# A hybrid decoder layer on one core: output projection in three rounds, triangular solve in smaller steps, and other priorities for weight splits and bank evictions

## The chip, the cores and the metric

The kernel runs on one core of one Trainium2 chip. The metric is the device time of one execution in microseconds (us); the figure of a kernel is the median of its runs. One more execution was taken with the hardware profiler, and all rows below are of that one.

## The reference

One decoder layer for 256 tokens of width 2048, in float32:

```python
n = rmsnorm(x, attn_norm)
u = n @ w_in                                  # 6928 columns, cut into four groups
mix = concat[gated_deltanet(u_gdn), mlstm(u_mlstm), rglru_block(u_rglru), rwkv7(u_rwkv)]
x = x + mix @ w_out
n = rmsnorm(x, ffn_norm)
x = x + (silu(n @ ffn_w_gate) * (n @ ffn_w_up)) @ ffn_w_down
return rmsnorm(x, final_norm)
```

The four mixers are causal recurrences over the 256 tokens, each 512 wide with four heads (the RWKV-7 one with eight). GatedDeltaNet and RWKV-7 are computed in chunks, for which a unit lower triangular system is solved: here blocks of 32 x 32 are inverted by forward substitution, and the larger blocks are put together with small matmuls.

## The kernel before, in words

**Units.** All large weights are read in units of 128 x 1024 floats (512 KB), in the order in which they are used: 108 units of `w_in` (27 groups of 256 columns, four units each), 32 units of `w_out`, 176 of the gate and up weights and 88 of the down weights, 404 in all. I call them U0 to U403. For each unit `weights` (line 261) issues a DMA into one of 4 buffers `raw` on SP's queue, and `halves` makes from it, into one of 4 buffers each, `whi` (rounded, ScalarE) and `wlo` (the rest, VectorE). `mm3` (line 281) then multiplies in three passes: whi by the high half of the activation, whi by its low half, wlo by its high half. A unit of `w_in` takes 24 matmuls of 256 columns, all others 12 of 512 columns.

**Mixers beside the weights.** A mixer half is a Python generator (`rwkv_half`, `gdn_half`, `mlstm_half`, `rglru_half`), and so are `gates_mm` and the two solves (`joint_solve` over `solve_blocks`). After each unit `tick(TICKS)` adds 0.65 of a step, and at each whole step every living generator goes on to its next `yield`. So a `yield` is a place where the rest of a mixer is put later in program order, by about one and a half units. A generator that waits for another (`while "gdS" not in em.mix: yield`) asks again at each step. The finished output of a half stands in `em.mix[mixer, half]`.

**Order on the queues.** The order of each engine's queue isn't written by hand. A scheduler orders instructions by priority, which is the place in program order, lowered by an offset inside `high_priority(offset=...)`, and by when it thinks that their inputs and buffers are there. `weights` gives the DMA and both splits an offset of PRIO (20 instructions); functions marked `@evict` (`conv`, `silu2`, `shift_mix`, `gelu2`: the emptying of a PSUM bank of a group and what follows) have EPRIO (40); the mixers' matmuls and transposes go through `Lag`, which puts them 20 instructions later. On the chip each queue then runs in that fixed order.

**The output projection.** `w_out` (line 1181) computes four column quarters q of 512. For the quarter it takes the two banks of its 256 tokens, and for each `part` (a half of a mixer) one unit: if the part isn't split yet, it is split into a high and a low half (`split`, lines 1176 and 1177), then 12 matmuls follow and a tick. At the end the two banks are added to the residual `em.xq` (line 1211). There are two passes over the quarters: `early` with RWKV, RG-LRU and GatedDeltaNet (6 units per quarter, U108 to U131) and `late` with mLSTM (2 units per quarter, U132 to U139). While generators live, `bank` gives only the 3 banks `big`; afterwards it goes around all 8.

**Steps in program order around the change.** Counting ticks in the code: GatedDeltaNet's two halves are spawned behind U59 and U75, and the inputs of its solve are complete at U87. The solve `gds` has 31 columns of two VectorE instructions each, 8 columns to a step, and ends at U94. The halves go on and finish at U107 and U109. The second mLSTM half is spawned behind U107 and finishes at U117.

Of the kernel before, what the change touches and what calls it, by code (L numbers as in the profile page):

```python
# [23 lines left out]
TICKS = 0.65  # L24
LAG = 20
UNIT = 1024
PRIO = 20
EPRIO = 40
WARM = 14
TAIL = 3  # L30
HOLD = {("rw1", 17): 1, ("gates", 1): 1, ("rg0", 0): 1, ("rg1", 1): 3}
# [758 lines left out]
def gates_mm(em):  # L790
# [5 lines left out]
    z = em.mx()  # L796
# [47 lines left out]
    nc.vector.tensor_tensor_scan(M[0:4, 0:T], M[0:4, T : 2 * T], M[0:4, T : 2 * T], 0.0, op0=ALU.max, op1=ALU.max)  # L844
    em.Md = em.dp.tile([4, T], F32, name="Md", tag="Md")
    nc.sync.dma_start(em.Md, M[0:4, 0:T])
    t = em.mx()
    for a in range(2):
        em.pe.transpose(t[:, a * 4 : a * 4 + 4], M[0:4, a * P : a * P + P], em.ident[0:4, 0:4])
# [17 lines left out]
def gdn_half(em, hf, Q, K, V, SZ):  # L867
# [3 lines left out]
    for s, X, bias in ((1, Q, em.c_lnq), (0, K, 0.0)):  # L871
        silu2(em, X)
        sq = em.S()
        nc.scalar.activation(sq, X, AF.Square)
        z = yield from sums(em, em.onesr, sq)
        rsqrt_ln(em, sq, z, em.c_4eps, ebias=bias)
        nc.vector.tensor_tensor(KQv[:, s, :], X, sq, op=ALU.mult)
        em.free(sq, X)
        yield
    silu2(em, V)  # L880
    z = em.mx()
# [25 lines left out]
    for g in range(2):  # L907
        z = em.mx()
# [132 lines left out]
def mlstm_half(em, hf, Q, K, V1, SO, v1s):  # L1041
    nc = em.nc
    silu2(em, Q)
    silu2(em, K)
    while "gates" not in em.mix:
        yield
    zb = bcast_rows(em, em.Md, hf)
    yield
    Hs = em.S(c="B")
    ss = em.const([P, 2, 2], em.nm("mss"))  # L1050
    rs = em.const([P, 2, 2], em.nm("mrs"))
    for g in range(2):
        hd = 2 * hf + g
        E = em.S(c="B")
        nc.vector.tensor_scalar(E[:, 0:T], zb[:, g * T : g * T + T], em.c[:, 0, hd : hd + 1], 0.0, op0=ALU.subtract, op1=ALU.max)
        nc.vector.tensor_scalar(E[:, T : T + P], zb[:, g * T + P : g * T + T], em.c[:, 1, hd : hd + 1], 0.0, op0=ALU.subtract, op1=ALU.max)
        nc.scalar.activation(E[:, 0 : T + P], E[:, 0 : T + P], AF.Exp, scale=-1.0)
        Ed = E.rearrange("p (b n) -> p b n", n=T)[:, :, 0:P]
        nc.vector.tensor_tensor(Ed, Ed, em.incl.unsqueeze(1).to_broadcast([P, 2, P]), op=ALU.mult)
        z = em.mx()  # L1060
        em.pe.matmul(z[:, 0:T], K[:, g * T : g * T + P], Q[:, g * T : g * T + T], start=True, stop=True)
        em.pe.matmul(z[:, T : T + P], K[:, g * T + P : g * T + T], Q[:, g * T + P : g * T + T], start=True, stop=True)
        nc.vector.scalar_tensor_tensor(E[:, 0 : T + P], z[:, 0 : T + P], 0.25 * 128.0**-0.5, E[:, 0 : T + P], op0=ALU.mult, op1=ALU.mult)
        yield
        z = em.mx()
        sq = Seq(em)
        sq.mm(z[:, 0:129], E[:, 0:P], V1[:, 0, g, :], start=True, stop=True)
        sq.mm(z[:, 129:258], E[:, P:T], V1[:, 0, g, :], start=True, stop=False)
        sq.mm(z[:, 129:258], E[:, T : T + P], V1[:, 1, g, :], start=False, stop=True)
        em.free(E)  # L1070
        dn = em.const([P, 2], em.nm("dn"))
        zv = z[:, 0:258].rearrange("p (a n) -> p a n", a=2)
        nc.scalar.activation(dn, zv[:, :, 128], AF.Abs)
        nc.vector.tensor_tensor(dn, dn, em.enm[:, :, hd], op=ALU.max)
        nc.vector.reciprocal(dn, dn)
        junk = em.S(c="B")
        for a in range(2):
            o = slice(g * T + a * P, g * T + a * P + P)
            nc.vector.scalar_tensor_tensor(Hs[:, o], zv[:, a, 0:P], dn[:, a : a + 1], SO[:, a * T + g * P : a * T + g * P + P], op0=ALU.mult, op1=ALU.mult)
            nc.scalar.activation(junk[:, 0:P], Hs[:, o], AF.Square, accum_out=ss[:, g, a : a + 1])  # L1080
        em.free(junk)
        nc.vector.tensor_scalar(ss[:, g], ss[:, g], 1.0 / 128, EPS, op0=ALU.mult, op1=ALU.add)
        nc.gpsimd.tensor_tensor(rs[:, g], ss[:, g], em.mhalf[:, 0:2], op=ALU.pow)
        for a in range(2):
            o = slice(g * T + a * P, g * T + a * P + P)
            nc.scalar.activation(Hs[:, o], Hs[:, o], AF.Copy, scale=rs[:, g, a : a + 1])
        yield
    em.free(Q, K, zb, v1s, SO)
    z = em.mx()
    for u in range(4):  # L1090
        em.pe.transpose(z[:, u * P : u * P + P], Hs[:, u * P : u * P + P], em.ident)
    for g in range(2):
        nc.scalar.activation(Hs[:, g * T : g * T + T], z[:, g * T : g * T + T], AF.Copy, scale=em.PT["mlstm_norm"][:, 2 * hf + g : 2 * hf + g + 1])
    em.mix["ml", hf] = Hs
# [83 lines left out]
    return hi, lo  # L1178


def w_out(em):
    nc, A = em.nc, em.A
    xin = A["x"].rearrange("(a p) d -> p a d", p=P)
# [6 lines left out]
    row = {"gd": 0, "ml": 4, "rg": 8, "rw": 12}  # L1190
    sp = {}

    def run(q, parts):
        banks = [em.bank(), em.bank()]
        for i, (m, hf) in enumerate(parts):
            if (m, hf) not in sp:
                while (m, hf) not in em.mix:
                    em.tick()
                sp[m, hf] = split(em, em.mix[m, hf])
                em.free(em.mix[m, hf])  # L1200
            hi, lo = (t.bitcast(F32R) for t in sp[m, hf])
            whi, wlo = em.weights("w_out", row[m] + 2 * hf, 2, q * 512, 512)
            for a in range(2):
                for kk in range(2):
                    ts = slice(kk * T + a * P, kk * T + a * P + P)
                    em.mm3(banks[a], hi[:, ts], lo[:, ts], whi[:, kk, :], wlo[:, kk, :], start=i == 0 and kk == 0, stop=i == len(parts) - 1 and kk == 1)
            em.tick(TICKS)
            if q == 3:
                em.free(*sp[m, hf])
        for a in range(2):  # L1210
            nc.vector.tensor_tensor(em.xq[a, q], em.xq[a, q], banks[a], op=ALU.add)

    early = [(m, h) for m in ("rw", "rg", "gd") for h in range(2)]
    late = [("ml", 0), ("ml", 1)]
    for q in range(4):
        run(q, early)
    ss = em.const([P, 2, 4], "ss1")

    def norm(q):
# [4 lines left out]
            em.free(junk)  # L1224

    for q in range(4):
        run(q, late)
        if q:
            norm(q - 1)

# [124 lines left out]
def hybrid(tc, A, out, dbg=None, parts=("rw", "gd", "ml", "rg", "tail", "ffn")):  # L1355
    nc = tc.nc
    with ExitStack() as ctx:
# [50 lines left out]
        if "gd" in parts:  # L1408
            for hf in range(2):
                z = grp(GD + 1536 + 256 * hf, tm=True)  # L1410
                SZ = em.S(c="L")
                with em.tc.high_priority(offset=EPRIO):
                    for a in range(2):
                        nc.scalar.activation(SZ[:, a * T : a * T + T], z[:, a * T : a * T + T], AF.Copy, scale=em.rs0[:, a : a + 1])
                silu2(em, SZ)
                Q, K, V = (conv(em, grp(GD + 512 * i + 256 * hf), em.PT["gdn_conv"], 12, (4 * i + 2 * hf, 4 * i + 2 * hf + 1)) for i in range(3))
                em.spawn(f"gd{hf}", gdn_half(em, hf, Q, K, V, SZ))
                if hf == 0:
                    em.spawn("gds", joint_solve(em, "gd", 64, 32, 8, True))
        if "ml" in parts:  # L1420
            for hf in range(2):
                v1s = em.S(2)
# [40 lines left out]
```

## Time and profile before

| | |
|---|---|
| median of 3 runs | 1279.06 us (1278.2 to 1281.37) |
| the profiled execution, own time | 1279.74 us |
| its span, first to last instruction | 1278.0 us |
| TensorE matmul (PE) busy | 1246.7 us, 98% |
| TensorE weight load (PEld) busy | 1077.1 us, 84% |
| VectorE (DVE) busy | 781.3 us, 61% |
| ScalarE (ACT) busy | 636.3 us, 50% |
| mean granted TensorE clock | 0.986 |

The span runs from the first to the last instruction; the own time has 1.7 us more around it. Busy is time in which an engine has an instruction running. Matmuls are pipelined, so that the spacing of their starts, not their duration, is what one costs. L276 is line 276 of the kernel; where a helper passes calls on, many instructions share its line (L276 for what `ch` calls, L401 and L405 for the mixers' matmuls and transposes). [...]

### The profile page before, as it was taken

To read this page: it belongs to the slowest core of one execution; us is meant where nothing else is said; L and a number is where in the kernel's file an instruction comes from. 1 tells how busy PE (TensorE), PEld (TensorE's weight loads), DVE (VectorE), ACT (ScalarE), POOL (GpSimd) and SP (SyncE) were. 2 spreads that over 40 slices of the span, in tenths; PEclk is the share of its full clock that TensorE was granted. 3 is DMA by queue.
4 is the path that set the end of the run, shared out by engine and by line. 5 is a ranking of instruction groups with operands and counts; after the bars stand their busy time and mean duration, and the time that the engine had idled before them with its cause. 6 is when DMAs were issued, how large, how long until landed. Compare 5 with 4: busy or idle time off the path is not lost.

```text
span 1278.0 us, 18349 instructions
## 1 busy us (share of the span) xinstructions
PE 1246.7 (98%) x7216; PEld 1077.1 (84%) x7216; DVE 781.3 (61%) x1082; ACT 636.3 (50%) x846; POOL 31.6 (2%) x65
## 2 busy tenths in 40 slices
PE   9999999999989799999999999999999999999997
PEld 8999999888989688888888888888888888878885
DVE  7676899567798665754444454444454455557554
ACT  7566675517634354644444444444444454445443
POOL 2000000000000100000000000000000000001000
PEclk9999999989999899999999999999999999999999
DMA  9644446234644246666666665666566666666663
GB/s 371 215 129 136 158 124 175 93 120 165 196 145 141 94 149 192 183 181 187 195 188 187 187 196 186 208 199 196 184 194 190 189 185 194 195 191 189 193 190 112
DMA packets 72198, 226.97 MB, mean 178 GB/s; under 512 B 15752, under 2 KB 16016, under 8 KB 72112
## 3 DMA queue, kind: packets, MB, share of 16 engines
q1 hardware_dynamic: 71504, 224.14, 57.0%
q0 software_dynamic: 464, 1.57, 0.4%
q8 instruction: 56, 0.92, 0.3%
q14 instruction: 30, 0.25, 0.1%
q10 hardware_dynamic: 144, 0.10, 0.0%
HBM read 222.49 MB, written 3.28 MB: 177 GB/s over the span
## 4 chain that ended last, share of the span: by engine, by line
PE 87%; DVE 7%; ACT 3%; issue 2%; DMA 1%; POOL 0%; SPq 0%; DVEq 0%; POOLq 0%; ACTq 0%
PE big L171 13%; PE big L170 13%; PE big L169 13%; PE mx L169 10%; PE mx L171 10%; PE mx L170 10%; PE mx L401 4%; PE mxl L171 3%; PE mxl L170 3%; PE mxl L169 3%; DVE wlo L276 2%; PE big L279 2%; DVE sD L494 1%; DVE sD L495 1%; DVE sA L759 1%
## 5 line engine op out<-in xcount | busy, mean ns | idle before, releaser
L276 DVE TENSOR_TENSOR wlo<-raw,whi 128x1024 fp32r<-128x1024 f32 x396 | 485.0, 1227 | 373.5 <-ACT whi L276 371.6
L276 ACT ACTIVATE whi<-raw 128x1024 fp32r<-128x1024 f32 x396 | 418.0, 1057 | 459.9 <-PE big L171 266.9
L171 PE MATMUL big<-nhi,wlo 128*128 128x256 f32 x608 | 176.6, 291 | 1.0 <-DVE wlo L276 1.0
L170 PE MATMUL big<-nlo,whi 128*128 128x256 f32 x608 | 176.5, 290 | 0.0
L169 PE MATMUL big<-nhi,whi 128*128 128x256 f32 x608 | 175.9, 289 | 0.2 <-ACT whi L276 0.2
L170 PE MATMUL big<-wlo,nhi 128*128 128x512 f32 (+1 forms) x464 | 161.8, 349 | 0.0
L171 PE MATMUL big<-whi,nlo 128*128 128x512 f32 (+1 forms) x464 | 161.4, 348 | 0.0
L169 PE MATMUL big<-whi,nhi 128*128 128x512 f32 (+1 forms) x464 | 161.2, 347 | 0.0
L169 PE MATMUL mx<-whi,nhi 128*128 128x512 f32 x352 | 138.0, 392 | 0.0
L171 PE MATMUL mx<-whi,nlo 128*128 128x512 f32 x352 | 137.0, 389 | 0.0
L170 PE MATMUL mx<-wlo,nhi 128*128 128x512 f32 x352 | 137.0, 389 | 0.0
L171 PEld LDWEIGHTS big<-nhi,wlo 128*128 128x128 f32 x608 | 117.6, 194 | 3.5 <-DVE wlo L276 1.2
L170 PEld LDWEIGHTS big<-nlo,whi 128*128 128x128 f32 x608 | 117.5, 193 | 2.8 <-issue 1.3
L169 PEld LDWEIGHTS big<-nhi,whi 128*128 128x128 f32 x608 | 117.4, 193 | 2.6 <-issue 0.7
L170 PEld LDWEIGHTS big<-wlo,nhi 128*128 128x128 f32 x464 | 88.9, 192 | 10.9
L169 PEld LDWEIGHTS big<-whi,nhi 128*128 128x128 f32 x464 | 88.7, 191 | 10.8
L171 PEld LDWEIGHTS big<-whi,nlo 128*128 128x128 f32 x464 | 88.7, 191 | 10.7
L169 PE MATMUL mx<-whi,sA 128*128 128x512 f32 x212 | 82.9, 391 | 0.7 <-ACT sA L1176 0.7
L170 PE MATMUL mx<-wlo,sA 128*128 128x512 f32 x212 | 82.5, 389 | 0.0
L171 PE MATMUL mx<-whi,sA 128*128 128x512 f32 x204 | 79.4, 389 | 0.0
L171 PEld LDWEIGHTS mx<-whi,nlo 128*128 128x128 f32 x352 | 66.1, 188 | 13.8
L170 PEld LDWEIGHTS mx<-wlo,nhi 128*128 128x128 f32 x352 | 66.1, 188 | 13.3
(432 smaller groups left out, 1703.3 us busy)
## 6 DMA issues: line engine op xcount, KB each, us to landing
raw<-in_units SPq DMA_DIRECT2D x404, 512.0 KB, 3.7
sD<-in_x SPq DMA_DIRECT2D x8, 512.0 KB, 7.8
sD<-in_xT SPq DMA_DIRECT2D x4, 512.0 KB, 6.1
out_y<-sD SPq DMA_DIRECT2D x8, 256.0 KB, 3.0
sA<-in_final_norm POOLq DMA_DIRECT2D x4, 256.0 KB, 5.1
sD<-in_lora SPq DMA_DIRECT2D x1, 512.0 KB, 7.1
sD<-in_rglru POOLq DMA_DIRECT2D x1, 512.0 KB, 7.6
dr<-sD SPq DMA_DIRECT2D x2, 256.0 KB, 4.0
```

Source lines behind the costliest of these rows:

```text
L169: i = nc.tensor.matmul(out, ahi, bhi, start=start, stop=False, skip_group_check=True)
L170: nc.tensor.matmul(out, ahi, blo, start=False, stop=False, skip_group_check=True)
L171: self.last_mm = nc.tensor.matmul(out, alo, bhi, start=False, stop=stop, skip_group_check=True)
L276: i = fn(*a, **k)
L279: i = fn(*a, **k)
L401: return self.em.nc.tensor.matmul(*a, **k)
L494: nc.vector.tensor_tensor(tv, col, row, op=ALU.mult)
L495: nc.vector.tensor_tensor(inv[:, j + 1 : n, 0:b], inv[:, j + 1 : n, 0:b], tv, op=ALU.add)
L759: nc.vector.scalar_tensor_tensor(o[:, d:T], u[:, 0 : T - d], tap[3 - d], o[:, d:T], op0=ALU.mult, op1=ALU.add)
```

## The change

Two constants; one more `yield` in `gates_mm`, in `mlstm_half` and (through `sums(..., 1)`) twice in each `gdn_half`; the GatedDeltaNet solve with 4 columns to a step in place of 8; and `w_out` in three passes (rounds) over the quarters in place of two: first RWKV and RG-LRU (4 units per quarter, U108 to U123), then mLSTM (U124 to U131), then GatedDeltaNet (U132 to U139). A part is now split one part ahead of its use, in the last quarter of a round also the first part of the next round.

```diff
-PRIO = 20
-EPRIO = 40
+PRIO = 200
+EPRIO = 100
...
     nc.sync.dma_start(em.Md, M[0:4, 0:T])
+    yield
     t = em.mx()
...
         nc.scalar.activation(sq, X, AF.Square)
-        z = yield from sums(em, em.onesr, sq)
+        z = yield from sums(em, em.onesr, sq, 1)
...
     zb = bcast_rows(em, em.Md, hf)
-    yield
+    for _ in range(2):
+        yield
...
+ROUNDS = ([("rw", 0), ("rw", 1), ("rg", 0), ("rg", 1)], [("ml", 0), ("ml", 1)], [("gd", 0), ("gd", 1)])
...
-    def run(q, parts):
+    def ready(m, hf):
+        if (m, hf) not in sp:
+            while (m, hf) not in em.mix:
+                em.tick()
+            sp[m, hf] = split(em, em.mix[m, hf])
+            em.free(em.mix[m, hf])
+
+    def run(q, r):
+
+        parts = ROUNDS[r]
         banks = [em.bank(), em.bank()]
         for i, (m, hf) in enumerate(parts):
-            if (m, hf) not in sp:
-                while (m, hf) not in em.mix:
-                    em.tick()
-                sp[m, hf] = split(em, em.mix[m, hf])
-                em.free(em.mix[m, hf])
+            ready(m, hf)
+            if i + 1 < len(parts):
+                ready(*parts[i + 1])
+            elif q == 3 and r + 1 < len(ROUNDS):
+                ready(*ROUNDS[r + 1][0])
...
-    early = [(m, h) for m in ("rw", "rg", "gd") for h in range(2)]
-    late = [("ml", 0), ("ml", 1)]
-    for q in range(4):
-        run(q, early)
+    for r in range(len(ROUNDS) - 1):
+        for q in range(4):
+            run(q, r)
...
     for q in range(4):
-        run(q, late)
+        run(q, len(ROUNDS) - 1)
...
-                    em.spawn("gds", joint_solve(em, "gd", 64, 32, 8, True))
+                    em.spawn("gds", joint_solve(em, "gd", 64, 32, 4, True))
```

## Rows read from the trace of the kernel before

**Rows 1.** The page, part 1: busy us (share of the span) x instructions.

```profile
PE 1246.7 (98%) x7216; PEld 1077.1 (84%) x7216; DVE 781.3 (61%) x1082; ACT 636.3 (50%) x846; POOL 31.6 (2%) x65
```

**Rows 2.** Busy time by stretch: length, engines (x instructions), PEclk, DMA share, GB/s.

```profile
54.30:254.00 199.70, 197.68 (x1701) 184.95 (x1700) 155.96 (x285) 124.49 (x180) 3.07 (x5) 0.99 0.46 141
...
254.00:280.00 26.00, 24.80 (x183) 20.84 (x182) 18.30 (x38) 5.34 (x10) 0.00 (x0) 0.80 0.26 79
280.00:305.80 25.80, 25.80 (x252) 23.37 (x251) 15.21 (x25) 11.66 (x17) 0.10 (x1) 1.00 0.70 236
305.80:336.00 30.20, 27.25 (x206) 26.43 (x206) 25.32 (x42) 27.79 (x38) 0.00 (x0) 0.94 0.37 121
...
374.80:424.50 49.70, 44.76 (x415) 42.57 (x413) 41.03 (x86) 18.66 (x34) 1.53 (x2) 0.97 0.52 155
424.50:443.60 19.10, 11.67 (x68) 10.33 (x69) 11.77 (x35) 7.97 (x27) 2.23 (x3) 0.80 0.17 56
...
448.00:514.40 66.40, 66.31 (x303) 54.75 (x303) 41.03 (x55) 32.26 (x47) 1.38 (x2) 1.00 0.57 174
...
538.80:1264.00 725.20, 724.52 (x3246) 600.80 (x3244) 374.31 (x343) 332.10 (x371) 9.99 (x9) 1.00 0.63 189
```

**Rows 3.** Timeline of PE around the end of `w_in` (start, us, instruction, idle before).

```profile
424.06 0.28 PE L170 MATMUL big<-nlo,whi 128*128 128x256 f32 x1
424.17 0.28 PE L171 MATMUL big<-nhi,wlo 128*128 128x256 f32 x1
424.47 0.68 PE L401 MATMUL mx<-sL,sB 64*64 64x64 f32 x8
...
443.30 0.69 PE L405 MATMUL mx<-ident,sB 128*128 128x128 f32 x2 [2.25 <-DVE sB L994]
443.65 0.78 PE L169 MATMUL big<-whi,sA 128*128 128x512 f32 x1
```

**Rows 4.** Timeline of ACT in the same stretch.

```profile
431.50 0.38 ACT L1005 ACTIVATE sA<-mx 128x256 f32<-128x256 f32 x1 [5.27 <-PE mx L401]
...
439.39 0.63 ACT L1176 ACTIVATE sA<-sB 128x512 fp32r<-128x512 f32 x1 [3.33 <-DVE sA L452]
```

**Rows 5.** Timeline of DVE: the solve's first and last instruction, and a late eviction.

```profile
354.21 0.18 DVE L494 TENSOR_TENSOR sD<-sD,sD 32x31 f32<-32x31 f32 x1
...
405.89 0.18 DVE L495 TENSOR_TENSOR sD<-sD,sD 32x31 f32<-32x31 f32 x1
...
438.69 0.68 DVE L452 TENSOR_TENSOR sA<-big,sA 128x512 f32<-128x512 f32 x1
```

**Rows 6.** Groups by line: names, shapes, count | busy us, mean ns | idle before.

```profile
L276 DVE TENSOR_TENSOR wlo<-raw,whi 128x1024 fp32r<-128x1024 f32 x396 | 485.0, 1227 | 373.5 <-ACT whi L276 371.6 <-DMA sB<-Md 0.3 <-issue 0.2
...
L495 DVE TENSOR_TENSOR sD<-sD,sD 64x31 f32<-64x31 f32 (+31 forms) x62 | 20.5, 331 | 1.2
```

**Rows 7.** The chain that ended last: one group of four mixer transposes (start, us).

```profile
107.48 0.44 PE mx L405 x4
```

**Rows 8.** Busy time by stretch of the instructions on the `big` banks alone.

```profile
254.00:280.00 26.00, 14.63 (x77) 11.84 (x76) 0.69 (x1) 0.00 (x0) 0.80 0.26 79
280.00:305.80 25.80, 20.40 (x144) 17.96 (x143) 0.69 (x1) 0.00 (x0) 1.00 0.70 236
```

**Rows 9.** Waits of SP's queue from 6 to 515 us (total us, times, longest).

```profile
SPq L276 <- DVE wlo L276: 271.2, 91, 16.2
```

**Rows 10.** Waits of PE from 6 to 448 us: the one for a VectorE split.

```profile
PE big L171 <- DVE wlo L276: 1.0, 1, 1.0
```

**Rows 11.** Groups of DVE by line from 217 to 305 us.

```profile
L713 DVE SCALAR_TENSOR_TENSOR sB<-mx,sc,sB 64x64 f32<-64x64 f32 x16 | 4.5, 283 | 0.4
L696 DVE COPY sD<-mx 64x256 f32<-64x256 f32 x8 | 3.4, 428 | 8.3 <-PE mx L401 8.2
L691 DVE COPY sB<-mx 64x256 f32<-64x256 f32 x8 | 3.4, 427 | 4.5 <-PE mx L401 4.4
```

**Rows 12.** Waits of ACT from 224 to 448 us.

```profile
ACT whi L276 <- PE big L170: 42.5, 15, 11.9
```

## The prediction

> **What bounds the kernel now.** I read the page's part 1 first: PE is busy for 98% of the span [rows 1], so what can be won is time in which PE runs something other than weights at full pace. The busy table by stretch says where that is [rows 2]. From 538.8 to 1264 us, the feed-forward part, PE is busy for 724.5 of 725.2 us at clock 1.00, with 3246 matmuls, 0.223 us each, and VectorE and ScalarE about half idle: nothing to win there, and little to lose. From 448 to 514.4 us it is the same. The loss lies before 448 us. The largest piece is the stretch 424.5 to 443.6 us: PE runs 68 instructions in 19.1 us, is busy for 11.7, and the granted clock is 0.80. The timeline of PE shows what stands there [rows 3]: the last matmul of `w_in` starts at 424.17 us, then come only mixer matmuls (L401, L405), and the first matmul of `w_out` starts at 443.65 us. The timeline of ACT says why [rows 4]: the split of the first part of `w_out` (L1176) runs at 439.39 us, although its input (RWKV) is finished some 30 units earlier in program order; it stands on ACT behind an instruction of GatedDeltaNet's recurrence (L1005) that waited 5.27 us for PE, and then waits itself for an eviction (L452) that VectorE gets to only at 438.69 us [rows 5]. So GatedDeltaNet's chain runs by itself at the end, and what could cover it queues behind it. It comes so late because its solve holds VectorE from 354.21 to 405.89 us [rows 5], 51.7 us for 20.5 us of work (2 x 31 instructions by 331 ns [rows 6]), while VectorE is busy for 41.0 of the 49.7 us from 374.8 us on [rows 2].
>
> Smaller losses: from 254 to 280 us PE has 1.2 us idle and a clock of 0.80; from 374.8 to 424.5 us 4.9 us idle and 0.97; from 305.8 to 336 us 2.95 us idle, with ACT busy for 27.8 of 30.2 [rows 2].
>
> **Order of `w_out`, with the solve in smaller steps and the added steps.** Counted in ticks, the added steps and the 7 in place of 3 yields of the solve move the end of GatedDeltaNet from U107/U109 to U117/U118, and that of the second mLSTM half from U117 to U118. The use moves further: GatedDeltaNet from U112 to U131/U132, three units of cover before, 13 or more after; mLSTM from U132 to U123/U124, five units or more of cover. A unit of `w_out` is 12 matmuls by 0.223, 2.7 us. So behind the last group there are 16 units of RWKV and RG-LRU, 43 us of matmuls whose inputs have long been there, and the splits now stand in program order ahead of GatedDeltaNet's last steps. Of the 19.1 us I count what is not the mixers' own PE work. Bound from below: idle time alone, 19.1 - 11.7 = 7.4. From above: 68 mixer instructions at 0.11 us each (0.44 for four transposes [rows 7]) are 7.5, which leaves 11.6. [...] The same covering in the stretch from 374.8 on: idle 4.9, and 0.03 x 49.7 = 1.5 of clock; between 0 and 6.4, since the mixers' matmuls there wait for a VectorE that stays as full as it was. I take **4**: the recurrences and the solve's small matmuls, which end that stretch, move behind U108.
>
> **Splits 200 instructions ahead.** A unit is 24 matmuls, one DMA, two splits and some mixer steps, so 20 instructions are less than one unit, and 200 are more than the four buffers can hold. From now on every split goes ahead of any mixer work, up to four units early. Where it can pay is shown from 254 to 280 us: the `big` banks get 77 matmuls there, against 144 in the next 25.8 us [rows 8], with 183 - 77 = 106 and 252 - 144 = 108 mixer instructions beside them [rows 2, 8]. Weights at 0.12 us a matmul [rows 3] are 9.2 of the 26.0 and 17.3 of the 25.8; the 108 mixer instructions thus cost at most 8.5 in the second stretch, and 26.0 - 9.2 - 8.5 = 8.3 are lost in the first. Bounds 0 and 8.3. I take **3**, under the middle: much of that stretch is a chain of recurrences that goes to VectorE and back, and a split standing ready fills PE's wait only where the scheduler put its matmuls there. From 305.8 to 336 us ACT is nearly full; between 0 and 2.95, I take **1**.
>
> The cost of the same edit: a split takes 1227 ns of VectorE [rows 6], and a mixer instruction that is overtaken waits that long. It is hidden as long as PE has weights to multiply; if that cover is gone, it is the third rival. The DMAs move too: on SP's queue a unit's DMA waits for `wlo` to free its buffer (271.2 us in 91 waits [rows 9]), and the mixers' DMAs stand behind it. One such wait lasts about a unit, 2.9 us (24 x 0.12); the chain through the solve has two DMA hops, and the cover of 13 units holds that.
>
> **The rest.** Evictions at 100 instead of 40: behind the splits now, which costs them at most four splits (4.9 us); with three banks one is needed again two groups later (8 units, 23 us), so nothing. Three rounds add 8 additions into `xq` of about 0.68 us (L452 has the same shape [rows 5]), 5.4 us of a VectorE that is busy for 41.0 of 66.4 us there [rows 2]: nothing on PE, except that a bank may come free late; I take **1** against, between 0 and 5.4. Splitting one part ahead costs nothing, it moves 1.3 us of work earlier. Up to 254 us the order changes too. PE is idle there for 2.0 of 199.7 us, at clock 0.99 [rows 2], so at most 4.0 can be won; what can be lost no row shows but the third rival's, and I put 0, with 4 either way.
>
> **Sum.** 11 + 4 + 3 + 1 - 1 = 18 off the profiled execution's own 1279.74 us is 1261.7. Its own time is 0.7 over the median of 1279.06, so against the runs I give **1261**. With all upper ends, 11.6 + 6.4 + 8.3 + 3.0 and 4 of the early stretch, 33.3 come off the median: 1246. With the lower ends alone, 7.4 off and 5.4 and 4 on, it is 1281, which is a rival's place.
>
> **Rivals.** (1) *The splits' priority does nothing.* In the stretches that count four units may be split already, so only the order of `w_out` acts: 11 + 4 - 1 off, 1265; if the part before 424.5 us stays as it is, 1269. For it: PE's one wait for a VectorE split up to 448 us lasted 1.0 us [rows 10]; it waited for mixer operands. Against: at 254 us VectorE was behind with them.
>
> (2) *The gap only moves.* mLSTM's second half is spawned behind U107 and is now needed at U124 instead of U132. Its last eviction ran at 438.69 us on a full VectorE; if that queue is as late after the change, PE waits at U124 for what it waited for at U108. Price: the 11 come back, and what is left is within 4 us of before, 1277 to 1281. Against: 43 us of cover.
>
> (3) *Slower: splits stand in front of the recurrence.* From 217 to 305 us RWKV-7 goes PE, VectorE, PE for each chunk; VectorE's part are 8 + 8 copies (L691, L696) and 16 updates (L713) in 8 groups or fewer [rows 11], some 24 handovers. ACT already stood waiting with a split at its head, for PE to free a buffer, 42.5 us in 15 waits, the longest 11.9 [rows 12]. If each handover waits for one more `wlo` of 1.227 us [rows 6] and PE has nothing in its queue between, that is 29 on, less the 15 of `w_out`: 1293. It decides where PE's program order there holds mixer matmuls back to back without weights between them. [...] Against: the table of stretches shows VectorE only 15.2 of 25.8 us busy from 280 us on [rows 2], room enough.
>
> (4) *Splits far ahead take over.* If PE never lacks a weight, all small losses before 424.5 us go as well: the upper ends, 1246.
>
> **Chances.** My forecast, with (4) as its far end: 0.57. Rival (1): 0.23. Rival (2): 0.08. Rival (3): 0.12. A measurement of this kernel can tell about 0.3% (3.8 us) from no change. Faster by more: 0.57 + 0.23 = 0.80; within: 0.08; slower: 0.12. The range goes from 1242, a little under the upper ends, to 1278, which takes in a part of (2); it leaves out (3), the rest of (2), and some 0.03 below.
>
> **What would show it.** Right: the matmuls of `w_out` follow those of `w_in` within 2 us, with L401 between them and not alone; L1176 of RWKV runs before the last GatedDeltaNet steps; the clock stays at 1.00 in that stretch; the solve's instructions lie between weight splits up to about U110; the stretch 538.8 to the end is as long as before. For the splits: no stretch in which `wlo` starts less than 3 us before its matmuls, and the 26 us from 254 get more than 77 matmuls into `big`. Wrong: PE idle at U124 or U132 with mLSTM or GatedDeltaNet as releaser (2); L691 or L696 with more than the 8.2 us of waits and PE waiting for them (3); or stretches before 374.8 us as long as before (1). A feed-forward part longer than before would be something that I have not thought of.

## The result, and the profile after

The changed kernel takes **1283.0 us** (median of 9 runs, 1282.8 to 1286.1) beside 1276.5 for the kernel before in 9 runs of the same set: ratio 1.0051, interval [1.0034, 1.0067]. It is slower by half a per cent, where I forecast 1261 (1242 to 1278). The profiled execution took 1284.88 us.

Part 1 of the page of the kernel after answers to [rows 1]: PE does the same 7216 matmuls.

```profile
PE 1243.5 (97%) x7216; PEld 1072.6 (84%) x7216; DVE 786.5 (61%) x1090; ACT 642.5 (50%) x849; POOL 30.8 (2%) x65
```

The stretches of [rows 2] no longer hold the same work. So I cut both kernels where PE starts the same unit: U0, U16, U60, U76, U108 (the first of `w_out`), U120, U140 (the first of the feed-forward part). First the kernel before, PE alone (stretch: length, busy, instructions, PEclk, DMA share, GB/s). PEclk is the share of the full TensorE clock that was granted, as a mean over the stretch: in the kernel before it is 0.50 from 262 to 268 us and 1.00 from 284 to 288.

```profile
6.90:54.30 47.40, 47.35 (x388) 1.00 0.85 315
...
217.20:305.80 88.60, 87.40 (x873) 0.94 0.43 134
305.80:443.60 137.80, 121.03 (x987) 0.95 0.46 140
443.60:481.80 38.20, 38.10 (x175) 0.97 0.44 133
...
538.80:1278.00 739.20, 729.46 (x3267) 1.00 0.62 188
```

The same units in the kernel after:

```profile
6.90:64.90 58.00, 50.74 (x389) 0.91 0.76 266
...
228.10:310.50 82.40, 82.40 (x873) 1.00 0.51 151
310.50:428.70 118.20, 103.90 (x824) 0.96 0.51 152
428.70:481.90 53.20, 51.78 (x332) 0.97 0.38 114
...
540.20:1283.00 742.80, 731.43 (x3267) 0.99 0.63 187
```

Read from the top: U0 to U16 **loses 10.6 us**. U60 to U76 gains 6.2. U76 to U108 gains 19.6, but it has 163 instructions fewer, and its idle time (length less busy) only went from 16.8 to 14.3. Then U108 to U120 **gives 15.0 back**, with 157 instructions more: mixer work that moved. The feed-forward part **loses 3.6**. The two stretches left out differ by 0.3 and 1.3.

PE's waits from 6 to 520 us name the two longest (total, times, longest): four transposes of mLSTM ahead of U108, and the first scale.

```profile
PE mx L405 <- ACT sA L1088: 5.9, 1, 5.9
PE mx L269 <- POOL rs L350: 5.6, 1, 5.6
```

The timeline of PE before the first matmul of `w_out` answers to [rows 3]. It starts at 428.73 in place of 443.65 us, and only eight mixer matmuls stand alone ahead of it, but both still wait:

```profile
422.56 0.28 PE L171 MATMUL big<-nhi,wlo 128*128 128x256 f32 x1
425.73 0.60 PE L401 MATMUL mx<-sB,sB 32*32 32x32 f32 x8 [2.89 <-DMA sB<-dr]
428.73 0.79 PE L169 MATMUL big<-whi,sA 128*128 128x512 f32 x1 [2.40 <-ACT sA L1178]
```

VectorE's timeline of the solve answers to [rows 5]: it now takes 58.3 us in place of 51.9 and ends at 418.50.

```profile
360.41 0.18 DVE L494 TENSOR_TENSOR sD<-sD,sD 32x31 f32<-32x31 f32 x1
...
418.50 0.18 DVE L495 TENSOR_TENSOR sD<-sD,sD 32x31 f32<-32x31 f32 x1
```

**The start.** L269 makes the first scale from the row sums of squares of x; all evictions behind it need that. The loads of x go out on SP's queue. Its timeline in the kernel before (start, us, L255 is the load of x):

```profile
15.66 0.94 SPq L255 DMA_DIRECT2D sD<-in_x  x2
18.00 0.34 SPq L276 DMA_DIRECT2D raw<-in_units  x1
18.39 1.61 SPq L255 DMA_DIRECT2D sD<-in_x  x2
20.36 18.80 SPq L276 DMA_DIRECT2D raw<-in_units  x6
```

And after, where seven weight loads went ahead, which took 14.6 us, 13.7 of them waits (SP's waits from 15.6 to 30.3 us):

```profile
15.61 14.59 SPq L276 DMA_DIRECT2D raw<-in_units  x7
...
33.46 1.33 SPq L255 DMA_DIRECT2D sD<-in_x  x2
36.47 0.34 SPq L276 DMA_DIRECT2D raw<-in_units  x1
36.85 1.13 SPq L255 DMA_DIRECT2D sD<-in_x  x2
```

PE's timeline of the kernel after shows what follows, a wait and then a first eviction that comes late:

```profile
48.44 1.22 PE L269 MATMUL mx<-ident,rs 128*128 128x128 f32 x4 [5.59 <-POOL rs L350]
50.99 0.55 PE L169 MATMUL big<-nhi,whi 128*128 128x256 f32 x1 [1.33 <-DVE sA L452]
```

These waits are 6.9 of the 10.6 us; beside them PE ran at a lower granted clock, 0.91 over the stretch in place of 1.00.

### The profile page after: what moved, and what is told of

Same layout as the page of the kernel before. It is cut to its first block, busy times and chain, and to the rows that moved or that the text cites. A ratio compares the mean times of both kernels' runs of the same rounds, so it can differ in the third digit from the quotient of the medians.

```text
span 1283.2 us, 18364 instructions
## 1 busy us (share of the span) xinstructions
PE 1243.5 (97%) x7216; PEld 1072.6 (84%) x7216; DVE 786.5 (61%) x1090; ACT 642.5 (50%) x849; POOL 30.8 (2%) x65
## 4 chain that ended last, share of the span: by engine, by line
PE 88%; DVE 6%; ACT 2%; issue 2%; DMA 1%; POOL 0%; DVEq 0%; SPq 0%; POOLq 0%; ACTq 0%
PE big L171 14%; PE big L169 14%; PE big L170 14%; PE mx L171 10%; PE mx L169 10%; PE mx L170 10%; PE mx L401 4%; PE mxl L171 3%; PE mxl L169 3%; PE mxl L170 3%; DVE wlo L276 2%; PE big L279 2%; ACT whi L276 1%; PE mx L405 1%; DMA sD<-in_x 1%
## 5 line engine op out<-in xcount | busy, mean ns | idle before, releaser
L276 DVE TENSOR_TENSOR wlo<-raw,whi 128x1024 fp32r<-128x1024 f32 x396 | 484.7, 1225 | 377.3 <-ACT whi L276 376.2
L276 ACT ACTIVATE whi<-raw 128x1024 fp32r<-128x1024 f32 x396 | 418.8, 1058 | 463.6 <-PE big L171 267.4
L171 PE MATMUL big<-whi,nlo 128*128 128x512 f32 (+1 forms) x448 | 154.3, 344 | 0.0
L170 PE MATMUL big<-wlo,nhi 128*128 128x512 f32 (+1 forms) x448 | 154.1, 344 | 0.0
L169 PE MATMUL big<-whi,nhi 128*128 128x512 f32 (+1 forms) x448 | 154.1, 344 | 0.0
L169 PEld LDWEIGHTS big<-whi,nhi 128*128 128x128 f32 x448 | 84.8, 189 | 10.2
L170 PEld LDWEIGHTS big<-wlo,nhi 128*128 128x128 f32 x448 | 84.8, 189 | 10.1
L171 PEld LDWEIGHTS big<-whi,nlo 128*128 128x128 f32 x448 | 84.8, 189 | 10.1
```

Of the source, the lines that this page charges most:

```text
L169: i = nc.tensor.matmul(out, ahi, bhi, start=start, stop=False, skip_group_check=True)
L170: nc.tensor.matmul(out, ahi, blo, start=False, stop=False, skip_group_check=True)
L171: self.last_mm = nc.tensor.matmul(out, alo, bhi, start=False, stop=stop, skip_group_check=True)
L276: i = fn(*a, **k)
```

## The experiments

| kernel | us, median (range, runs) | ratio to before, interval |
|---|---|---|
| `a1` before, units' offset 200 | 1290.2 (1287.8 to 1293.0, 6) | 1.0112 [1.0093, 1.0131] |
| `a2` before, evictions' offset 100 | 1278.3 (1274.1 to 1287.7, 12) | 1.0027 [1.0003, 1.0051] |
| `a3` after, both offsets as before | 1268.5 (1267.7 to 1269.1, 6) | 0.9941 [0.9926, 0.9956] |
| `a4` after, loads of x first | 1276.9 (1275.2 to 1278.6, 12) | 1.0001 [0.9989, 1.0013] |
| `b1` `a4`, feed-forward part at 20 | 1273.0 (1271.5 to 1276.4, 12) | 0.9973 [0.9959, 0.9988] |
| `b2` after, units' DMAs at 20 | 1274.4 (1271.6 to 1275.5, 12) | 0.9984 [0.9974, 0.9995] |
| `e1` `b2`, feed-forward part at 20 | 1269.8 (1269.2 to 1272.0, 6) | 0.9945 [0.9928, 0.9961] |
| `e2` after, scaling on VectorE | 1286.0 (1284.7 to 1287.2, 6) | 1.0067 [1.0049, 1.0084] |
| `b3` before, rounds alone | 1275.5 (1271.3 to 1278.7, 12) | 0.9987 [0.9973, 1.0001] |
| `c1` before, gates' yield alone | 1275.3 (1271.6 to 1281.8, 10) | 0.9992 [0.9972, 1.0012] |
| `c2` before, sums' yield alone | 1265.2 (1263.0 to 1266.6, 4) | 0.9903 [0.9876, 0.9929] |
| `c4` before, all steps, no rounds | 1275.4 (1273.7 to 1277.4, 12) | 0.9987 [0.9973, 1.0000] |
| `d1` `c2`, spread solve | 1276.0 (1274.1 to 1278.2, 11) | 1.0000 [0.9989, 1.0012] |
| `d2` `c2`, mLSTM's yield | 1279.3 (1277.3 to 1280.5, 11) | 1.0023 [1.0012, 1.0035] |
| `d3` `c2`, rounds | 1264.3 (1259.0 to 1264.5, 5) | 0.9896 [0.9877, 0.9914] |
| `d4` `d3`, early splits of `w_out` | **1259.0** (1257.5 to 1260.4, 4) | 0.9865 [0.9847, 0.9883] |
| `b4` `a3`, mLSTM's second yield, early splits | 1264.3 (1262.9 to 1266.3, 6) | 0.9911 [0.9892, 0.9929] |
| `c3` `b4`, two more steps in GatedDeltaNet | 1265.7 (1263.5 to 1266.3, 5) | 0.9905 [0.9881, 0.9928] |

### The offsets against the rest

`a1` and `a2` each set one constant of the kernel before, `a3` both of the kernel after:

```diff
-PRIO = 20          # a1
+PRIO = 200
-EPRIO = 40         # a2
+EPRIO = 100
-PRIO, EPRIO = 200, 100   # a3, from the kernel after
+PRIO, EPRIO = 20, 40
```

> The kernel before with the weights' priority at 200 instructions and nothing else. Theory A (the priority costs at two places, the loads of x on SP's queue and the turn between the halves of the last matrix, some 10 and 4 us, and wins some 8 in the recurrences): the wait of PE before L269 appears (5 us or more, U16 starts near 64 us instead of 54), the last matrix loses 3 to 4 us, time 1279 to 1285. Theory B (the loss is that of the rounds and added steps, the priority is neutral): no wait before L269, 1274 to 1279.

> The kernel before with the priority of bank evictions at 100 and nothing else. Theory A and theory B both expect less than 0.3% from before, 1273 to 1280; if evictions are what comes late before w_out (L452 at 438.69 us in the kernel before), the gap of 19.1 us shrinks and it is 1262 to 1270.

> The changed kernel with both priorities back at 20 and 40: the three rounds, the solve in steps of 4 and the added steps alone. Theory A: the start is as before (U16 near 54 us), the gap before w_out shrinks by some 10 us, time 1264 to 1272. Theory B: the gap only moves or grows, 1276 to 1285.

The units' offset alone (the DMA and both splits) makes the kernel before slower by 1.1%, 5 us beyond the end of theory A's range; taking both offsets out of the kernel after turns its loss into a gain of 0.6%. The evictions' offset is at the edge of what can be told.

### Which queue, and which place

`a4` puts only the loads of x into the same priority; `b2` takes only the units' DMAs out of it:

```diff
-        nc.sync.dma_start(xs..., self.A["x"]...)      # a4
+        with self.tc.high_priority(offset=PRIO):
+            nc.sync.dma_start(xs..., self.A["x"]...)
-        with self.tc.high_priority(offset=PRIO):       # b2
-            return self.halves(self.raw(*key), *key)
+        with self.tc.high_priority(offset=20):
+            raw = self.raw(*key)
+        with self.tc.high_priority(offset=PRIO):
+            return self.halves(raw, *key)
```

`b1` is `a4`, and `e1` is `b2`, with 20 for units whose name begins with `ffn`.

> The changed kernel, with the four pairs of loads of x for the sum of squares at the same priority as the weights (200) and everything else as in the changed kernel. Theory A: the loads go out by 25 us, the wait before L269 goes, U16 starts near 54 us, 8 to 11 us less than the changed kernel, 1271 to 1276. Rival (the splits ahead on ScalarE and VectorE, not SP's queue, made the sum of squares late): the wait before L269 stays above 4 us, 1280 to 1285.

> The kernel after, with the offset of 200 for the two splits of a unit alone; its DMA goes back to 20. Theory A (at the start it is the order on SP's queue, not the order of ACT and VectorE, that makes PE wait): the loads of x go out as early as before, no wait before L269, U16 at about 55 us, and the time falls by the 6 us of the loads, to 1277 (1274 to 1279); the rest of the offset's cost, which is at the splits, stays. Theory B (the splits at 200 by themselves hold up the squares of x on ACT and VectorE): the wait before L269 stays at 4 us or more and the time is within 2 of 1283. If also the 4.7 us in the mixers' stretch that are still open come from mixer loads behind weight loads, it goes under 1273.

> The kernel after, with the four loads of x ahead of the weights' loads and, beside that, an offset of 20 again for the feed-forward part's units; the units of w_in and w_out keep 200. Theory A (the offset of 200 costs at two places, SP's queue at the start and the turn between the two halves of the down projection, and the rest of it is neutral): the 6.2 us that the loads alone gave back and 3.7 at the turn (1.93 us of a wait and about 1.8 of half clock) both come off 1283.0, so 1273 (1271 to 1275), without a wait of over 1 us for whi or wlo at 1147 to 1160 us. Theory B (the loss at the turn comes from the evictions' offset or from VectorE sharing with GpSimd, not from the offset of the splits): the wait of 1.9 us stays and the time is that of the loads alone, 1277 (1275.5 to 1278.5). Either way some 4 us should still lie above the 1268.5 of the rounds at the old offsets, in the stretch of the mixers.

> The kernel after with the loads of the units at 20, the splits at 200 up to the end of w_out, and the feed-forward part's splits at 20. Beside the rounds and steps at the old offsets (1268.5) this is the splits' priority alone, for which the forecast had a gain of 4 us. Theory A (the splits' priority does nothing for the mixers' stretch: there PE waits for the mixers' operands and not for weights): 1268 to 1271, the stretch up to U140 within 1 us of 528.1. Theory B (it wins as forecast): 1263 to 1266. Theory C (it costs in the recurrences too, which the 1274.4 with the feed-forward part at 200 leaves room for): 1271 to 1273.

With the loads of x first the wait before L269 is gone and 6.2 us with it: the order on SP's queue is shown to make that wait. Part of the loss at the start stays, since PE starts U16 at 58.1 us in `a4`, not near 54 as theory A had it, and the time lies 0.9 over theory A's range. With all units' DMAs at 20 (`b2`) U16 starts at 54.7 and 8.6 us are won: the whole loss there is the DMAs' order. PE then starts U140 at 528.5 us, against 528.1 in `a3`: on top of the new steps and rounds, splits at 200 cost and win nothing up to there. What `b2` still loses to `a3` lies behind U140 (741.3 us in place of 739.3 in the profiled executions; that of `b2` is the fastest of its 12). Putting the feed-forward part back to 20 wins 3.9 us in `b1` and 4.6 in `e1`, which is then within 1.3 of `a3`. Theory A held in `b2`, `b1` and `e1`, and in `a4` for the wait but not for the time.

At the turn between the halves of the down projection, the kernel after has this wait (PE's waits from 1140 to 1165 us):

```profile
PE mx L171 <- DVE sA L1179: 1.8, 1, 1.8
```

Behind it, from 1154 to 1160 us, PE ran at a granted clock of 0.72; the kernel before has neither that wait nor a clock under 1.00 there. Three splits ran beside GpSimd's multiplication there, at 1765 ns each, as VectorE's groups from 1140 to 1160 us show (names, shapes, count | busy us, mean ns):

```profile
L1179 DVE TENSOR_TENSOR sA<-sD,sA 128x512 fp32r<-128x512 f32 x3 | 5.1, 1765 | 0.0
```

`e2` moves the multiplication to VectorE (L1342: `nc.gpsimd` becomes `nc.vector`).

> The kernel after with one edit: the four multiplications by the final norm's weights between the halves of the down projection run on VectorE in place of GpSimd. In the kernel after, three splits (L1179) that ran beside GpSimd's multiplication took 5.14 us there, 1.7 each, while one takes 0.69 elsewhere. Theory A (the two engines hold each other up, and that makes PE wait 1.93 us): the splits take 0.69 each, the wait of PE before L171 at 1152 us goes below 0.7, and the time falls by 2 to 4, to 1279 to 1281. Theory B (the place of the splits in VectorE's order makes the wait): the wait stays at 1.5 us or more, or grows, since the four multiplications at about 0.7 us now stand on VectorE itself; 1282 to 1286.

Now no split takes over 0.7 us (line 1179 of `e2`: least, median and greatest ns), yet PE waits longer there, 2.5 us, and the kernel is no faster:

```profile
L1179 DVE TENSOR_TENSOR sA<-sD,sA x45: 685/694/695, 484.9 to 1259.5; 128x512 fp32r<-128x512 f32 x45
```

```profile
PE mx L171 <- DVE sA L1179: 2.5, 1, 2.5
```

So a split does take longer beside GpSimd's multiplication, 1765 ns in place of 694, but PE's wait stays without that, as theory B had it. `e2` alone doesn't settle it, since it gives VectorE the four multiplications too. `b2` and `e1` do, which differ only in the offset of the feed-forward part's splits. VectorE's timeline at the turn, first `b2`, then `e1` (L278 is `wlo`, L1181 the split):

```profile
1139.56 1.23 DVE L278 TENSOR_TENSOR wlo<-raw,whi 128x1024 fp32r<-128x1024 f32 x1
1140.70 5.15 DVE L1181 TENSOR_TENSOR sA<-sD,sA 128x512 fp32r<-128x512 f32 x3
```

```profile
1139.36 0.68 DVE L1181 TENSOR_TENSOR sA<-sD,sA 128x512 fp32r<-128x512 f32 x1
1139.97 1.22 DVE L278 TENSOR_TENSOR wlo<-raw,whi 128x1024 fp32r<-128x1024 f32 x1
1141.10 3.48 DVE L1181 TENSOR_TENSOR sA<-sD,sA 128x512 fp32r<-128x512 f32 x2
```

In `e1` two splits are as slow beside GpSimd (3.48 us), and no wait of PE there is over 0.7 us. The difference is the first split: in `b2` a unit's `wlo` went ahead of it, it started 1.2 us later behind the last addition and ran beside GpSimd itself, and PE waited 1.8 us for it. The order on VectorE makes the wait: 1.2 us of the delay are the `wlo`, 1.1 the slower split.

### Rounds and steps

`b3` is the kernel before with the new `w_out` and nothing else. `c4` has the four step edits without it; `c1`, `c2`, `d1` and `d2` have these of them:

```diff
     nc.sync.dma_start(em.Md, M[0:4, 0:T])
+    yield                                            # c1, c4
-        z = yield from sums(em, em.onesr, sq)
+        z = yield from sums(em, em.onesr, sq, 1)     # c2, c4, d1, d2
-joint_solve(em, "gd", 64, 32, 8, True)
+joint_solve(em, "gd", 64, 32, 4, True)               # c4, d1
     zb = bcast_rows(em, em.Md, hf)
-    yield
+    for _ in range(2):                               # c4, d2
+        yield
```

> The kernel before with the new w_out (three rounds, splits one part ahead) alone: no added yields, the solve with 8 columns to a step, offsets 20 and 40. With all of them but the offsets it took 1268.5. Theory A (the order of w_out is what wins, since RWKV and RG-LRU stand ready for 16 units): within 2 us of that, 1267 to 1271, with PE's work going on from w_in to w_out without the stretch of 19 us. Theory B (the solve's smaller steps and the added steps carry part of the gain, by letting the splits of weights in between): 1271 to 1276, and the stretch from 374.8 us on loses more than it did with them.

> The kernel before with the four added yields and the solve in steps of 4 columns, and the old w_out in two passes and the old offsets. With the rounds it is 1268.5; the rounds alone gave 1275.5. Theory A (steps and rounds each win what the other does not): the 9 us of U64 to U68 are won, but GatedDeltaNet, needed at U112 and by its steps finished at U117, makes PE wait there: U108 to U140 takes 105 to 115 us in place of 95, and the time is 1272 to 1282. Theory B (the steps carry the gain, the rounds add little): 1266 to 1271.

> The kernel before with one edit: the added yield in the gates' generator. With all added steps and the rounds at the old offsets, U64 to U68 takes 28.0 us in place of 37.1 (from 230 to 267 us), and the granted clock there is 1.00 in place of 0.63 in 256 to 270 us; with the rounds alone it stays at 37.1. Theory A (the gates' step put their chain through ACT and VectorE into RWKV's recurrence, and one step later it falls elsewhere): U64 to U68 falls to 29 (28 to 31) and the kernel gains 2 to 10 us, 1267 to 1275. Theory B (it is GatedDeltaNet's step in its sums): U64 to U68 stays at 36 or more, the time is within 3 of 1277.

> The kernel before with one edit: the added yield in GatedDeltaNet's sums. Theory A (the gain between 230 and 267 us comes from the gates' yield): U64 to U68 stays at 36 or more us, the time within 3 of 1277. Theory B (it comes from this one): U64 to U68 falls to 29 (28 to 31), the granted clock in 256 to 270 us rises from 0.63 to over 0.9, and the time falls by 2 to 10 us, to 1267 to 1275.

> The kernel before with two edits: the yield in GatedDeltaNet's sums and the solve with 4 columns to a step. The sums' yield alone takes 1265.2; with the other three steps it is 1275.4, 10 more, of which 6.4 is one wait of PE in front of a transpose of mLSTM (L405). Theory A (the spread solve costs: its column operations stand between mLSTM's short operations on VectorE, 0.3 to 0.4 us each, and GatedDeltaNet finishes seven steps later, with fewer units behind it): 1272 to 1276, with a wait of over 5 us before L405 near 390 us. Theory B (mLSTM's added yield costs): within 3 of 1265.

> The kernel before with two edits: the yield in GatedDeltaNet's sums and the one more yield in mLSTM. Theory A (the spread solve costs the 10 us): within 3 of the 1265.2 of the first edit alone, no wait of over 3 us before L405. Theory B (the yield in mLSTM costs them, by moving the first half's chain beside a solve that fills VectorE): 1270 to 1276, with the wait before L405. If both this and its sister stay near 1265, the two edits cost only together.

My theory A of `b3` fell: the rounds alone are worth 1.7 us, which its interval does not tell from nothing, and the first matmul of `w_out` still starts as late as 441.2 us. One line of the change carries the gain, the yield between the squares of GatedDeltaNet's sums and the matmuls on them. `c1` gave nothing that can be told, `c2` 11 us by the medians and 12.4 by the ratio. ACT's timeline of the kernel before shows the place, with `whi` (L276) behind four table loads from 241.9 us on, of which the last two are shown:

```profile
247.15 1.28 ACT L481 ACT_TABLE_LOAD   x1
248.44 0.69 ACT L481 ACTIVATE sA<-mx,cv 128x512 f32<-128x512 f32 x1
249.15 1.28 ACT L899 ACT_TABLE_LOAD   x1
...
251.28 1.04 ACT L276 ACTIVATE whi<-raw 128x1024 fp32r<-128x1024 f32 x1
```

In `c2` a `whi` goes ahead of the second L481, behind two table loads:

```profile
247.66 1.04 ACT L276 ACTIVATE whi<-raw 128x1024 fp32r<-128x1024 f32 x1
```

What that does to PE (busy time by stretch, all engines; first the kernel before, then `c2`; PEclk is the third number from the end):

```profile
243.00:256.00 13.00, 12.82 (x146) 11.09 (x142) 9.03 (x26) 12.81 (x20) 0.11 (x1) 1.00 0.02 5
256.00:270.00 14.00, 13.14 (x71) 10.93 (x71) 6.89 (x14) 1.85 (x3) 0.00 (x0) 0.63 0.25 76
```

```profile
243.00:256.00 13.00, 13.00 (x140) 11.45 (x138) 7.77 (x17) 10.63 (x14) 0.11 (x1) 1.00 0.20 48
256.00:270.00 14.00, 12.29 (x137) 11.05 (x136) 11.08 (x25) 5.15 (x9) 0.00 (x0) 1.00 0.16 46
```

Before, ACT was full for 13 us, no weights came (DMA share 0.02), and then PE did 71 instructions at a clock of 0.63; in `c2` it does 137 at 1.00. U64 to U68 takes 27.6 us in place of 37.1. Not all of that is won. In `c1`, where ACT is as full (11.9 of 12 us from 240 to 252 us) and PE then idle for as long (1.0 us from 252 to 256 us, as in the kernel before from 254 to 258), it takes 33.2 at clock 1.00: so about 4 of the 9.5 are clock. And work moved, since U68 to U76 takes 42.3 in place of 38.4. The cuts of the section above, U60 to U76, U76 to U108 and U108 to U120, for `c2` (PE alone):

```profile
216.10:299.10 83.00, 81.29 (x872) 1.00 0.44 139
299.10:412.00 112.90, 104.97 (x888) 1.00 0.51 155
412.00:467.10 55.10, 53.41 (x272) 0.88 0.40 128
```

Over U60 to U76 5.6 us are left, and only 1.0 against the 84.0 of `c1`: in these executions nearly all of the gain there is clock. The larger part lies further on. From U76 to U120 `c2` takes 168.0 us in place of 176.0, and PE is idle for 9.6 of them in place of 16.9. Nearly 100 instructions moved from ahead of U108 behind it, among the matmuls of `w_out`, and the longest wait of the kernel before, 4.0 us for GatedDeltaNet's recurrence (L983), is gone. How one yield at U60 to U76 brings that about, no run takes apart.

The other steps cost: `d1` and `d2` each give all of it back. `d1` waits for the solve's DMA and for a split behind it, `d2` for mLSTM (PE's waits from 6 to 520 us, first `d1`, then `d2`):

```profile
PE mx L401 <- DMA sB<-dr: 3.8, 1, 3.8
...
PE big L169 <- ACT sA L1176: 2.4, 1, 2.4
```

```profile
PE mx L405 <- ACT sA L1087: 6.7, 1, 6.7
PE big L169 <- ACT sA L1177: 2.7, 2, 2.3
```

In `c2` no single wait of over 2 us is left. Together the costly edits take no more than each alone (`c4`).

### Mending the waits

`b4` is `a3` with a yield ahead of mLSTM's last transposes and `with em.tc.high_priority(offset=200)` around `split` in `w_out`; `c3` adds to it two yields ahead of the first matmul on the solved blocks (`range(4)` becomes `range(6)`).

> The rounds and steps at the old offsets (1268.5), with one more yield ahead of mLSTM's last four transposes and the splits of w_out's inputs 200 instructions ahead. There PE stood 6.4 us in front of a transpose (L405) that waited for ACT, with weights queued behind it, and later 3.0 in front of L401 and 2.8 in front of the first matmul of w_out. Theory A (these waits are places in PE's order, which one more step of 4.5 us takes away): the 6.4 goes to 2 or less, the 2.8 goes, and the time falls by 4 to 8, to 1261 to 1265. Theory B (the recurrences' chain is the bound there, so that a wait only moves to the next handover): the sum of PE's waits from 380 to 430 us stays within 2 us and the time at 1267 to 1270.

> The rounds and steps at the old offsets, with mLSTM's yield and the early splits (1264.3), and two more yields in GatedDeltaNet between the loads of the solved blocks and the first matmul on them (6 in place of 4). There PE waits 6.4 us in front of L401 for that DMA, and the clock stays at half from 406 to 417 us. Theory A (the wait is a place in PE's order): the wait goes to 1 us or less, with it some 4 us of half clock, and the time falls by 6 to 10, to 1254 to 1258. Theory B (the halves' last steps now come late): the wait goes, but PE waits as long for GatedDeltaNet's splits at U132, or for another handover; 1262 to 1266.

`b4` won 4 us, the low end of theory A, with two edits that it does not tell apart: the wait before L405 fell to 1.4, but the one for the solve's DMA grew to 6.4. `c3` won nothing, and the wait did not even go. PE's waits from 370 to 420 us, the solve's last instruction and the DMA on its result, in `c3`:

```profile
PE mx L401 <- DMA sB<-dr: 7.0, 1, 7.0
```

```profile
404.73 0.18 DVE L495 TENSOR_TENSOR sD<-sD,sD 32x31 f32<-32x31 f32 x1
```

```profile
408.71 0.32 SPq L943 DMA_DIRECT2D sB<-dr  x1
```

The solve ends at 404.73 and the load of its result starts at 408.71; PE stood there from 404.95, where it came to these matmuls at 403.95 in `b4`: two more yields did not move them behind another unit. Why the scheduler kept them there stays open.

`d3` joins the two edits that pay, `c2`'s yield and the rounds; `d4` adds the early splits of `b4`.

> The kernel before with two edits: the yield in GatedDeltaNet's sums (1265.2 alone) and w_out in three rounds (1275.5 alone, 1.6 under before). Theory A (they win at different places, 230 to 267 us and 424 to 444 us): the 1.6 comes on top, 1262 to 1265. Theory B (the rounds pay once the recurrences end earlier, as with all the steps, where they were worth 6.9): 1257 to 1261. Against both: the sums' yield already took U104 to U108 from 38.5 to 16.8 us, so that the rounds find nothing to cover: 1265 to 1267.

> The same two edits, and the splits of w_out's inputs 200 instructions ahead. Theory A (PE waits before the first matmul of w_out for a split that stands on ACT behind a recurrence): 1 to 3 us under its sister without this edit. Theory B (the split's input comes late itself): within 1 us of it.

The rounds add 0.9 us to the yield, which is within the intervals; the early splits add 5.2 by the medians and 4.0 by the ratios, more than theory A's 1 to 3, with intervals that still overlap. `d4` beats both kernels: 1259.0 us, 1.35% under the kernel before. Of its PE the stretches U76 to U108 and U108 to U120:

```profile
300.50:414.00 113.50, 106.42 (x889) 0.98 0.52 155
414.00:461.40 47.40, 47.24 (x273) 1.00 0.46 143
```

Idle time ahead of U108 is now 7.1 us, where it was 16.8 before and 14.3 after the change.

## Why the prediction was wrong

Differences of the ratios times 1276.5 us make one account, in the order in which the kernels build on each other, each good to some 2.5 to 4 us. In another order the parts differ: the rounds are worth 1.7 on the kernel before, 5.9 on `c4` and 0.9 on `c2`.

| part | from, to | us |
|---|---|---|
| the sums' yield | before, `c2` | -12.4 |
| the other three steps | `c2`, `c4` | +10.7 |
| the three rounds | `c4`, `a3` | -5.9 |
| splits up to U140 at 200, evictions at 100 | `a3`, `e1` | +0.5 |
| the feed-forward part's splits at 200 | `e1`, `b2` | +5.0 |
| the units' DMAs at 200 | `b2`, after | +8.6 |
| sum | before, after | +6.5 |

**The failed step: the DMAs on SP's queue.** I wrote that the mixers' DMAs stand behind a unit's DMA, "and the cover of 13 units holds that". I counted only those in the chain through the solve. The four loads of x stand on the same queue, at a place with no cover: everything behind L269 needs them. The row was there to be read, SP's timeline at 15.66 us. "Up to 254 us ... I put 0, with 4 either way" was 8.6.

**"Nothing to win there, and little to lose"** for the feed-forward part: 5.0 (2.2 between the profiled executions of `e1` and `b2`). An engine busy for 724.5 of 725.2 us has all to lose from a new order, and at the turn of the down projection a unit's matmuls take operands from two instructions on the same VectorE queue, `wlo` and the low half of the split.

**The splits' terms, 3 and 1:** nothing (`e1` against `a3`), as rival (1) has it. On the kernel before, the units' offset does shorten U60 to U76, from 88.6 to 80.1 us with 29 instructions fewer (`a1`), but U76 to U108 then takes 3.4 more; the sums' yield wins in the same place. The 8.3 us that I ascribed in 254 to 280 us to weights that were not ready were in good part clock: `c1`, with ACT as full there, takes 4.6 less from U60 to U76. The weights were late because ACT was full, 12.8 of 13.0 us from 243 us on, with four table loads of 1.28 us ahead of `whi`, and what takes these apart is a yield that I costed with the rest of the steps.

**The order of `w_out` with solve and steps, 11 + 4 - 1:** 7.6 together (`a3`), and from parts of either sign. I counted in ticks where each mixer ends and looked for cover at U124 and U132. No wait came there; the cover held. But it wasn't the order that closed the gap ahead of U108: from U104 to U108 the rounds alone leave 7.7 of the 9.0 us of idle time (`b3`), and the sums' yield leaves 1.7 with the old order (`c2`). And the other added steps also move what stands ahead of U108, where a recurrence's matmuls sit in PE's order with weights queued behind them: L405 waits 5.9, L401 2.9, the first matmul of `w_out` 2.4. So the idle time that I wanted covered changed its place. From U76 to U108 it was 16.8 us and is 14.3; of the 19.6 that the stretch got shorter, most is mixer work that now stands in the 15.0 behind U108. No run shows the 11, which was my estimate between 7.4 and 11.6: the rounds alone gave 1.7 us (`b3`), and on top of the steps 5.9 (`c4` to `a3`).

**Rival (2)**, that the gap only moves, was nearer than I gave it (0.08), though not to U124. **Rival (3)** had the sign and not the mechanism: from U60 to U76 the kernel after is 6.2 us faster. Of what stands ahead of what on ACT and VectorE, `e1` and `b2` show 0.5 us for the mixers, within the intervals, and 5.0 in the feed-forward part; on SP's queue the same cost most, 8.6 us (`b2`, after).

## What to carry to other kernels

A prefetch with a higher priority is a claim on every queue that it uses (on SP's it cost 8.6 us here): list everything else on that queue, DMAs above all, from its first use on, and ask of each who needs it and whether something covers it. A step added to a recurrence has no price of its own: one yield won 12 us and another lost 15, by what they put side by side, so try such steps one at a time. Judge a stretch by its idle time and not by its length: a stretch that got shorter may only have handed its work to the next.

## What the runs showed of the hardware

The stretch at half clock behind a wait of PE can be longer than the wait, and need not be there. Behind the 1.0 us wait of [rows 10], from 256 to 270 us, the kernel before ran at a granted clock of 0.63: it was 0.50 from 258.6 to 268.8 us, where weight matmuls of 256 columns started 0.21 us apart, beside 0.12 at a clock of 1.00 (284 to 288 us). In the profiled execution of `c1` PE was idle for 1.0 us at the same place (252 to 256 us), and the clock was 1.00 from 254 to 268 us. What decides between the two, no run here shows.

The spread of a kernel's executions goes with that clock. The kernel before was run 106 times beside the experiments, in 1272.6 to 1281.2 us. Where the mean granted clock was 0.993 it took 1272.6 to 1273.4 us, where it was 0.986 it took 1280.3 to 1281.2. The profiled execution that the prediction reads is one of 0.986, so a loss of clock in its rows need not be one of the median.

In the kernel after, VectorE and GpSimd were both slower beside each other at the turn of the down projection: a subtraction of two 128x512 tiles (L1179) took 1765 ns beside a GpSimd multiplication, and at most 695 with that multiplication gone (`e2`); of the multiplications (L1342) the three beside these subtractions took 5.08 us, 1.69 each, the first one, beside additions, 1.44. These additions with one input in PSUM (L276) took 683 ns beside it, and the one just ahead of it 0.69 us.
